# A hybrid attention and Fourier encoder on one core: banks of the reciprocal norms, request of x for the squares, place of a norm's product

## The chip, the core and the metric

The kernel runs on one core of a Trainium2 chip, as one program in one launch. TensorE (PE, with its weight loads on a row of their own, PEld), VectorE (DVE), ScalarE (ACT), GpSimd (POOL) and SyncE (SP) each work through their own list of instructions and wait for one another through semaphores. SP, POOL and ACT also issue the transfers between memory and the core; those wait in their issuer's list like any other instruction. The metric is the device time of one execution in microseconds, the median of several runs.

## What is computed

Two inputs of 1024 channels, one of 2048 tokens and one of 512, go through two layers and a final norm:

```python
def attention_layer(x, g, w_in, w_out, sink, rel_bias):
    h = rmsnorm(x, g)
    z = h @ w_in                       # q, k, v and gate in one projection
    ...
    o = banded_gqa_with_sink(q, k, v, rel_bias, sink)   # |i-j| <= 128, 16 heads, 4 kv heads
    return x + (o * jax.nn.silu(gate)) @ w_out

def fourier_layer(x, g, w_gate, w_out):
    h = rmsnorm(x, g)
    hg = h.astype(jnp.float32).reshape(b, s, N_FGROUPS, FGROUP_CH)
    f = jnp.fft.fftn(hg, axes=(1, 3), norm="ortho").real
    gate = h @ w_gate
    return x + (f.reshape(b, s, d) * jax.nn.silu(gate)) @ w_out
```

where `rmsnorm(x, g)` is `x * rsqrt(mean(x*x) + 1e-6) * g`. The sum of squares needs x with tokens on the partitions; the first projection needs x with channels there.

## The kernel before

**Products.** Operands are split into a high and a low part, and `matmul3` (line 92) multiplies high by high, high by low and low by high into one bank of accumulators (PSUM). All its matmuls show as line 95, whatever they compute; the tile names tell them apart: qp and gp (query and gate projections), op (output projection of attention), W, Z and X (gate products of the Fourier layer), z (transform over channels).

**Banks.** There are eight banks of 128x512 floats. In the attention phase four of them, `spt[0]` to `spt[3]`, are fixed and hold the scores; the other four rotate under the tag "bank" and are handed out by `bank(name)` (line 77) to qp, gp, pt, av, ib and op in turn. A tile that asks for a bank gets one of the four, and its first write waits until the previous holder has been read for the last time.

**Attention phase.** The tokens are worked through in five chunks of 512 (`CHUNKS`, line 35: first the sample's, then four of the prompt). For each chunk a loop over n = 0 to 16 (line 843) runs a pipeline over eight head pairs with two pairs of 128-query blocks each: scores of step n into `spt[:2]`, then into `spt[2:]` (line 468); DVE adds the bias and takes the minimum (`biased`, L487); ACT takes exponentials (L495); the weights are transposed (L527), copied out by ACT and DVE in two parts (`parts`, L535 and L536), and multiplied with the values in the next step (`av`, L553), whose result ACT and DVE take out (`out_evac`, L562 and L571). Pieces of the next projections are laid between as filler for TensorE. The order of PE, ACT and DVE in this loop is written out by `seq` and `pe`, which chain instructions; what isn't chained is placed by the planner that lays out the program, which takes instructions in the order in which they are written as far as its own estimate of the times has them ready.

The next chunk's reciprocal norms are made inside the same loop by `extra(i)` with i from 4n to 4n+3 (line 827):

- `stats(c)` (line 158) gives a list of steps that are taken at i = 38, 40, ... (from the second chunk on). Step `one(i)` squares the tile of x that step i-1 requested, on ACT with a running sum (L169), and requests tile i (L177). There are five tiles of 128 tokens for a chunk with a halo of 128 tokens, four for the last chunk. For chunks after the second (`c > 1`) the square is chained into ACT's order. The tiles have the tag "x", four buffers, shared with the weight sums that `EXTRA` makes up to i = 37 (w32e, e) and with the transposed x of the next chunk (xk, L212).
- `inv_rms` (line 86) makes the reciprocal roots with DVE and POOL.
- `spread(c, inv)` at i = 56, so in step n = 14, turns the column of 128 reciprocal norms of each tile into a row that is the same on all partitions: a PE transpose of the broadcast column per tile (L196) into a bank called ib, four tiles to a bank, and an ACT copy to `invb` per bank (L197). For the sample's chunk it uses `spt[0]` instead (`place`).

After the last gate projection of a chunk (`evac_g`, line 410: ACT tanh L413, DVE product L415, which is the last reader of gp's bank), step n = 14 holds av, then the spread, then the first four steps of `out_proj` (line 587), whose accumulator op takes a bank.

**Fourier phase.** The tokens are in twenty tiles, two to a `Pair`. The loop at line 1263 runs `gates(pr, hooks)` for one pair and, through the hooks, the transposes and transform of the next. For the pair after that one, x is loaded (L987), squared (L967), rooted (L88, L89) and multiplied in place by its reciprocal norm and by g (`norms`, line 989, the product at L992) at the head of each turn; the transposes L1000 read that product in the next turn. `z_odd_even` (line 1054) transforms the second tile of a pair: four banks, each read by an ACT copy (L1071) and by a DVE multiply-add (L1072). `z` (line 1035) then transforms the first tile into two further banks of the same pool of five. After every second pair, `combine` adds and subtracts four transforms on DVE (L1167).

Of the kernel before, what the change touches and what calls it, by code (L numbers as in the profile page):

```python
# [9 lines left out]
F32 = mybir.dt.float32  # L10
# [4 lines left out]
ALU = mybir.AluOpType  # L15
# [4 lines left out]
P = 128  # L20
D = 1024
# [21 lines left out]
def encoder(  # L43
# [3 lines left out]
    PE, ACT, DVE, POOL, SP = nc.tensor, nc.scalar, nc.vector, nc.gpsimd, nc.sync  # L47
# [29 lines left out]
    def bank(name):  # L77
        return banks[-1].tile([P, 512], F32, tag="bank", name=name)

    def xtile(shape, dtype, name):  # L80
        return xp.tile(shape, dtype, align_bytes=LINE, tag="x", bufs=4, name=name)
# [4 lines left out]
    def inv_rms(ss, n, name, place=lambda ins: None):  # L86
        inv = main.tile([P, 8], F32, tag="inv", bufs=2, name=name)
        place(DVE.tensor_scalar(inv[:, :n], ss[:, :n], 1.0 / D, EPS, ALU.mult, ALU.add))  # L88
        POOL.tensor_tensor(inv[:, :n], inv[:, :n], mhalf[:, :n], ALU.pow)  # L89
        return inv  # L90
# [44 lines left out]
    def after(ins, anchor):  # L135

        if anchor is not None:
            tc.add_manual_dep(ins.ins, anchor.ins.name, ISSUE, reason="issue order")

    def seq(engine, ins):  # L140

        after(ins, chain.get(engine))
        chain[engine] = ins
        return ins
# [4 lines left out]
    def attention_phase():  # L149

        with ExitStack() as es:
# [6 lines left out]
            def stats(c):  # L158

                tok, lo_t, hi_t = CHUNKS[c]  # L160
                nt = min(640, hi_t - tok) // P
                ss = main.tile([P, 8], F32, tag="ss", bufs=2, name=f"ss{c}")

                xs = []

                def one(i):

                    if i:
                        sq = ACT.activation(xs[i - 1], xs[i - 1], AF.Square, accum_out=ss[:, i - 1 : i])  # L169

                        if c > 1:
                            seq(ACT, sq)
                        else:
                            after(sq, last_exp[0])
                    if i < nt:
                        xs.append(xtile([P, D], F32, f"xs{c}_{i}"))
                        after(SP.dma_start(xs[i], x[tok + i * P : tok + (i + 1) * P, :]), last_exp[0])  # L177

                return [lambda i=i: one(i) for i in range(nt + 1)] + [
                    lambda: inv_rms(ss, nt, f"inv{c}", lambda ins: seq(DVE, ins) if c > 1 else None)  # L180
                ]

            def spread(c, inv, place=None):

                tok, lo_t, hi_t = CHUNKS[c]
                nt = min(640, hi_t - tok) // P
                if c:
                    invb = ap.tile([P, 640], F32, tag="invb", name=f"invb{c}")
                else:

                    invb = main.tile([P, 512], F32, tag="xr", bufs=3, name=f"invb{c}")
                for i0 in range(0, nt, 4):
                    m = min(4, nt - i0)
                    ps = bank(f"ib{c}_{i0}") if place is None else place
                    for i in range(m):
                        PE.transpose(ps[:, i * P : (i + 1) * P], inv[:, i0 + i : i0 + i + 1].to_broadcast([P, P]), ident)  # L196
                    ACT.copy(invb[:, i0 * P : (i0 + m) * P], ps[:, : m * P])  # L197
                return invb
# [39 lines left out]
            ps = bank("idle")  # L238
# [40 lines left out]
            spt = []  # L279
# [12 lines left out]
            last_exp, last_evac, last_mul, last_lo = [None], [None], [None], [None]  # L292
# [7 lines left out]
            def kv_proj(c, hs, halo, norms=None, early=None):  # L300
# [50 lines left out]
                for i0 in range(0, len(blocks), 4):  # L351
                    group = blocks[i0 : i0 + 4]
                    ps = [bank(f"vp{c}_{i0}_{i}")[:, :256] for i in range(len(group))]
                    for k in range(KD):
                        for i, (src, c0, b) in enumerate(group):
                            matmul3(ps[i], cols(src[k], c0, P), wslice(wv, k, 0, 256), k == 0, k == KD - 1)
                        if norms is not None and k == 4:

                            invb = spread(c, inv, spt[0])
                    for i, (src, c0, b) in enumerate(group):  # L360
                        v = ap.tile([P, 4, 2, HD], F32R, align_bytes=LINE, tag="v", bufs=6, name=f"v{c}_{b}")
                        vp = ps[i].rearrange("p (g d) -> p g d", g=4)
                        sc = 0.5
                        if inv is not None:
                            sc = ap.tile([P, 1], F32, tag="vsc", bufs=2, name=f"vsc{c}_{b}")
                            DVE.tensor_scalar(sc, inv[:, i : i + 1], 0.5, None, ALU.mult)
                        ACT.activation(v[:, :, 0, :], vp, AF.Copy, scale=sc)
                        DVE.scalar_tensor_tensor(v[:, :, 1, :], vp, sc, f32(v[:, :, 0, :]), ALU.mult, ALU.subtract)  # L368
                        vblk[b] = v
# [416 lines left out]
            for c in range(len(CHUNKS)):  # L786
# [33 lines left out]
                m = 15 * KD - ahead_n  # L820
# [6 lines left out]
                def extra(i):  # L827
                    nonlocal norm_steps, invb, inv
                    if c + 1 < len(CHUNKS):
                        if i == 24:  # L830
                            norm_steps = stats(c + 1)
                        if i >= (38 if c else 24) and i % (2 if c else 4) == 0 and norm_steps:
                            inv = norm_steps.pop(0)()
                        elif i == 56:
                            invb = spread(c + 1, inv)
                    if c in EXTRA and i in EXTRA[c]:
                        EXTRA[c][i]()
                    if c == len(CHUNKS) - 1 and i in AHEAD:
                        AHEAD[i]()
                    if c == 0 and i % 8 == 3 and 1 <= i // 8 < 3:  # L840
                        load_w(0, LATE[i // 8 - 1], f"late{i // 8}", late=last_exp[0])
# [76 lines left out]
    def fourier_phase(tail):  # L918
        with ExitStack() as es:
# [3 lines left out]
            gb = fp.tile([P, D], F32, tag="gb", bufs=1, name="g1b")  # L923
# [11 lines left out]
            def zt(name):  # L935
                return right([P, D], F32, name)
# [27 lines left out]
            def sumsq(src, name):  # L964
                ss = main.tile([P, 8], F32, tag="ss", bufs=2, name=f"ss{name}")
                junk = fp.tile([P, 512], F32, tag="c12", bufs=1, name=f"jk{name}").bitcast(BF16)
                ACT.activation(junk, src, AF.Square, accum_out=ss[:, 0:1])  # L967
                return inv_rms(ss, 1, f"inv{name}")
# [10 lines left out]
            class Pair:  # L979
# [9 lines left out]
                def norms(self, i):  # L989
                    xt = self.x[i]  # L990
                    inv = sumsq(xt, f"b{self.ts[i]}")
                    DVE.scalar_tensor_tensor(xt, xt, inv[:, 0:1], gb, ALU.mult, ALU.mult)  # L992

                def turn(self, i, hf):

# [58 lines left out]
                def z_odd_even(self):  # L1054

                    t = self.ts[1]
                    self.zs[1] = zt(f"z{t}")
                    for g in range(4):
                        ps = bank(f"z{t}_{g}")
                        for odd, m in enumerate((self.S[1], self.diff)):  # L1060

                            to = ps[:, odd * 256 : odd * 256 + 256].rearrange("p (a n) -> p a n", a=2)
                            for part in range(2):
                                PE.matmul(
                                    to, m[part][:, g * P : (g + 1) * P], ch[:, 0, :, odd * P : (odd + 1) * P],
                                    start=part == 0, stop=part == 1,
                                )
                        v = ps.rearrange("p (o a n) -> p a o n", o=2, a=2)
                        out = self.zs[1][:, g * 256 : g * 256 + 256].rearrange("p (n o) -> p o n", o=2)
                        scale = 1.0 if t >= SEQ // P else 0.5  # L1070
                        ACT.activation(out, v[:, 1], AF.Copy, scale=scale)  # L1071
                        DVE.scalar_tensor_tensor(out, v[:, 0], scale, out, ALU.mult, ALU.add)  # L1072

            def prod(out, a, b, ks, first):

# [492 lines left out]
            for i, l in enumerate((w0, w2)):  # L1568
                for a in range(3):
                    t = zt(f"ev{a}_{i}")  # L1570
# [5 lines left out]
            def pm(a, b, name):  # L1576

                n = zt(name)
                tt(n, a, b, A)
                tt(a, a, b, S)  # L1580
                return n, a
# [5 lines left out]
            f, g4s = pm(w0[1], w0[3], "f0")  # L1587
# [14 lines left out]
            for a in range(4):  # L1602
                for i, l in enumerate((pc, qs)):
# [3 lines left out]
                    t = zt(f"od{a}_{i}")  # L1607
# [170 lines left out]
```

## Time and profile before

| | |
|---|---|
| median of 3 runs | 1596.12 us (1593.97 to 1597.15) |
| the profiled execution | 1597.6 us, its span 1595.8 us |
| granted TensorE clock | 0.999 |
| attention phase, about | the first 1075 us of the span |
| Fourier phase, about | the rest |
| x requested for squares (L177) | 23 transfers of 512 KB, median 6.2 us from issue to landing |

The profile is one execution. PE is busy when a matmul is in the array; matmuls overlap, so the mean duration of one is longer than the distance from one to the next. In the timeline each row gives the start, the time over which a merged group ran, engine, line, operation, output and inputs with shapes, a count, and in brackets how long the engine had been idle before it and what ended that. "PE op L95 <- DVE s L415" in the view of waits is read as: TensorE, about to do line 95 into tile op, waited for DVE's line 415 on tile s.

### The profile page before, as it was taken

What the parts mean: (1) busy time and instruction counts of PE and PEld (TensorE: products, weight loads), DVE (VectorE), ACT (ScalarE), POOL (GpSimd) and SP (SyncE); (2) the same over time, 40 slices, a digit from 0 to 9 for tenths busy, and PEclk for the clock granted to TensorE, in tenths of its full rate; (3) what the DMA queues carried; (4) which work ended last, traced back from release to release, by engine and by line L of the source; (5) the groups of instructions that cost most, each with busy time, mean ns of one, the idle gap of its engine ahead of it and who ended that gap; (6) DMA issues with size and microseconds to landing.
All of it is one profiled execution on the core that took longest, in us unless ns stands there. A gap on an engine that the chain in (4) does not pass through costs nothing. (4 is left out here: it accounts for less than half of the span.)

```text
span 1595.8 us, 27413 instructions
## 1 busy us (share of the span) xinstructions
PE 1576.0 (99%) x9743; PEld 1320.9 (83%) x9743; DVE 1152.2 (72%) x2785; ACT 875.0 (55%) x2088; POOL 446.9 (28%) x613
## 2 busy tenths in 40 slices
PE   9999999999999999999999999999999999999998
PEld 7878788888888878988888888888888888888886
DVE  6788665887548775377764587769778878889796
ACT  6688534676237774257752476646555554243242
POOL 2466652421404314024223242123112111110110
PEclk9999999999999999999999999999999999999999
DMA  7598695565856566756659655675557469558762
GB/s 295 191 325 286 222 352 212 216 229 207 299 213 216 209 233 236 245 191 239 234 166 328 229 205 216 247 252 200 205 204 256 171 220 404 184 178 308 264 206 79
DMA packets 100579, 373.88 MB, mean 234 GB/s; under 512 B 12139, under 2 KB 22379, under 8 KB 83036
## 3 DMA queue, kind: packets, MB, share of 16 engines
q1 hardware_dynamic: 81708, 297.91, 53.0%
q0 software_dynamic: 16400, 70.04, 11.4%
q10 hardware_dynamic: 2336, 4.20, 0.7%
q8 instruction: 77, 1.26, 0.3%
q14 instruction: 58, 0.48, 0.1%
HBM read 280.84 MB, written 91.26 MB: 233 GB/s over the span
## 5 line engine op out<-in xcount | busy, mean ns | idle before, releaser
L487 DVE CUSTOM_DVE_ANT_0 S<-spt,b 128x385 f32<-128x385 f32 (+1 forms) x320 | 156.0, 527 | 113.7 <-PE spt L468 72.8
L95 PE MATMUL qp<-h,wq 128*128 128x512 f32 x960 | 237.4, 396 | 0.3 <-DVE v L368 0.2
L95 PE MATMUL gp<-h,wg 128*128 128x512 f32 x960 | 237.5, 395 | 0.0
L95 PEld LDWEIGHTS qp<-h,wq 128*128 128x128 f32 x960 | 174.9, 188 | 37.6 <-DVE v L368 0.8
L95 PEld LDWEIGHTS gp<-h,wg 128*128 128x128 f32 x960 | 174.9, 188 | 37.1 <-issue 1.0
L495 ACT ACTIVATE S<-S 128x385 f32<-128x385 f32 (+1 forms) x320 | 188.8, 597 | 19.1 <-DVE S L487 18.6
L535 ACT CAST pts<-pt 128x384 fp32r<-128x384 f32 (+1 forms) x240 | 100.4, 462 | 171.5 <-PE pt L527 163.9
L536 DVE TENSOR_TENSOR pts<-pt,pts 128x384 fp32r<-128x384 f32 (+1 forms) x240 | 114.6, 523 | 27.7 <-ACT pts L535 27.6
L577 POOL TENSOR_TENSOR uT<-o,uT 128x256 fp32r<-128x256 f32 x75 | 55.6, 741 | 245.2 <-ACT uT L576 245.2
L95 PE MATMUL op<-wo,uT 128*128 128x512 f32 x480 | 119.0, 392 | 3.0 <-DVE s L415 3.0
L95 PE MATMUL spt<-wo,uT 128*128 128x512 f32 x480 | 120.4, 391 | 0.0
L553 PEld LDWEIGHTS av<-pts,v 128*128 128x128 f32 x576 | 100.9, 188 | 23.2 <-DVE pts L536 2.9
L553 PE MATMUL av<-pts,v 128*128 128x512 f32 (+1 forms) x576 | 117.5, 343 | 1.7 <-DVE pts L536 1.0
L468 PE MATMUL spt<-kwin,qab 64*128 64x384 f32 (+1 forms) x960 | 118.5, 352 | 0.0
L95 PE MATMUL fo<-wo,tTu 128*128 128x512 f32 x480 | 115.3, 392 | 0.0
L95 PEld LDWEIGHTS op<-wo,uT 128*128 128x128 f32 x480 | 89.3, 188 | 22.3 <-DVE s L415 3.8
L95 PEld LDWEIGHTS spt<-wo,uT 128*128 128x128 f32 x480 | 89.1, 188 | 18.4
L507 DVE TENSOR_SCALAR S<-S 128x384 f32<-128x384 f32 (+1 forms) x192 | 97.8, 510 | 6.8
L95 PEld LDWEIGHTS fo<-wo,tTu 128*128 128x128 f32 x480 | 88.3, 188 | 17.2 <-ACT wo L1534 0.3
L468 PEld LDWEIGHTS spt<-kwin,qab 64*128 64x128 f32 x960 | 74.6, 186 | 28.4 <-issue 27.5
L573 POOL TENSOR_TENSOR o<-o,s 128x256 f32<-128x256 f32 x75 | 55.3, 738 | 132.3 <-DVE o L571 132.0
L527 PE MATMUL pt<-ident,S 64*128 64x64 f32 x1344 | 82.6, 222 | 0.0
(322 smaller groups left out, 3182.1 us busy)
## 6 DMA issues: line engine op xcount, KB each, us to landing
wo<-wsd SPq DMA_DIRECT2D x32, 1024.0 KB, 5.1
wq<-wsd SPq DMA_DIRECT2D x31, 1024.0 KB, 7.3
wg<-wsd SPq DMA_DIRECT2D x31, 1024.0 KB, 4.9
x<-x1d SPq DMA_DIRECT2D x40, 512.0 KB, 3.9
b<-b21d SPq DMA_DIRECT2D x40, 512.0 KB, 6.5
b<-rowd SPq DMA_DIRECT2D x40, 384.0 KB, 4.1
xs<-in_x_dram SPq DMA_DIRECT2D x23, 512.0 KB, 6.2
s2d<-gt POOLq DMA_DIRECT2D x40, 256.0 KB, 5.2
```

The lines of the kernel that those rows point to most:

```text
L95: pe(PE.matmul(out, a[i], b[j], start=start and i + j == 0, stop=stop and i == 1, skip_group_check=more))
L468: pe(PE.matmul(banks[j][:, 2 + k0 * P : 2 + k1 * P], res["q"][rows, qp, b * P : (b + 1) * P], kwin[g][rows, kp, b * P + k0 * P : b * P + k ...
L487: seq(DVE, DVE.tensor_tensor_reduce(out=s[:, e0:e1], in0=ps[:, 1 + e0 : 1 + e1], in1=st["bias"][:, j, 386 - e1 : 386 - e0][:, ::-1], scale ...
L495: last_exp[0] = seq(ACT, ACT.activation(s[:, e0:e1], s[:, e0:e1], AF.Exp, bias=s[:, 386:387], scale=-1.0, accum_out=s[:, 387:388]))
L507: seq(DVE, DVE.tensor_scalar(s[:, ks], s[:, ks], den, None, ALU.mult))
L527: pe(PE.transpose(ps[h][:, kb, j, :], ss[j][rows, 1 + kb * P : 1 + (kb + 1) * P], ident[rows, rows]))
L535: seq(ACT, ACT.copy(hi, ps[:, k0:k1]))
L536: seq(DVE, DVE.tensor_tensor(lo, ps[:, k0:k1], f32(hi), ALU.subtract))
L553: pe(PE.matmul(to, v, pt, start=n == part == 0, stop=part == 1 and n in (1, len(todo) - 1), skip_group_check=n > 1,))
L573: eng.tensor_tensor(o, o, s, ALU.mult)
L577: low = eng.tensor_tensor(lo, o, f32(hi), ALU.subtract)
```

## The change

Three edits.

1. `spread` no longer takes rotating banks. It cuts the tiles three and two (or three and one in the last chunk) instead of four and one, and writes them into columns 2 to 385 of `spt[3]` and `spt[2]`. The sample's chunk goes on as before.
2. In `stats`, for chunks after the second, the first step requests two tiles of x, and each later step requests the tile after the next, until all are requested.
3. In the Fourier phase the product L992 is placed on DVE behind the last L1072 that was written before it: an edge that orders two instructions of one engine and adds no semaphore.

```diff
-                    if i < nt:
-                        xs.append(xtile([P, D], F32, f"xs{c}_{i}"))
-                        after(SP.dma_start(xs[i], x[tok + i * P : tok + (i + 1) * P, :]), last_exp[0])
+                    while len(xs) < min(nt, i + (2 if c > 1 else 1)):
+                        t = len(xs)
+                        xs.append(xtile([P, D], F32, f"xs{c}_{t}"))
+                        after(SP.dma_start(xs[t], x[tok + t * P : tok + (t + 1) * P, :]), last_exp[0])
...
-                for i0 in range(0, nt, 4):
-                    m = min(4, nt - i0)
-                    ps = bank(f"ib{c}_{i0}") if place is None else place
+                step = 3 if place is None else 4
+                for i0 in range(0, nt, step):
+                    m = min(step, nt - i0)
+                    ps = spt[3 - i0 // 3][:, 2:386] if place is None else place
...
-                    DVE.scalar_tensor_tensor(xt, xt, inv[:, 0:1], gb, ALU.mult, ALU.mult)
+                    after(DVE.scalar_tensor_tensor(xt, xt, inv[:, 0:1], gb, ALU.mult, ALU.mult), last_z[0])
...
-                        DVE.scalar_tensor_tensor(out, v[:, 0], scale, out, ALU.mult, ALU.add)
+                        last_z[0] = DVE.scalar_tensor_tensor(out, v[:, 0], scale, out, ALU.mult, ALU.add)
+
+            last_z = [None]
```

## The prediction

> **What bounds the kernel now.** I read the page first: the engines, the granted clock in forty slices, and the projections' row of the costliest groups.
>
> ```profile
> span 1595.8 us, 27413 instructions
> PE 1576.0 (99%) x9743; PEld 1320.9 (83%) x9743; DVE 1152.2 (72%) x2785; ACT 875.0 (55%) x2088; POOL 446.9 (28%) x613
> PEclk9999999999999999999999999999999999999999
> L95 PE MATMUL qp<-h,wq 128*128 128x512 f32 x960 | 237.4, 396 | 0.3 <-DVE v L368 0.2
> ```
>
> TensorE is busy for 99% of the span at full clock in every slice, so the change, which takes no matmul away, can only give back time in which TensorE stood still: 1595.8 - 1576.0 = 19.8 us in all, its start and tail included. The last row gives the pace: 237.4 / 960 = 0.247 us from one 128x512 matmul to the next, though one lasts 0.396; a matmul that is held up therefore loses about 0.15 us more than the idle time shown. Next I read who TensorE, and then its weight loads, waited for, longest first.
>
> ```profile
> PE op L95 <- DVE s L415: 3.0, 3, 1.5
> PE z L95 <- DVE z L1072: 1.6, 2, 1.3
> PE av L553 <- DVE pts L536: 1.0, 3, 0.3
> PE W L95 <- DVE c L1138: 1.0, 1, 1.0
> PE av L553 <- ACT pts L535: 0.6, 3, 0.2
> ...
> PEld op L95 <- DVE s L415: 3.8, 3, 1.8
> PEld av L553 <- DVE pts L536: 2.9, 6, 0.7
> PEld av L553 <- ACT pts L535: 2.1, 4, 0.7
> PEld z L95 <- DVE z L1072: 2.0, 2, 1.5
> ```
>
> Three of these causes are touched: op behind s, av behind pts, z behind z. Together they are 3.0 + 1.6 + 1.0 + 0.6 = 6.2 us of PE's idle time, or 3.8 + 2.9 + 2.1 + 2.0 = 10.8 us of the weight loads'. The Trainium skill (Perfetto Trace Analysis, section Identifying the Most-Contended Engine) holds that matmul busy time misleads because matmuls are pipelined, and that the share of weight loads is to be read instead. By that rule the touched stalls are worth 10.8 us, by PE's own idle time 6.2; the sum below takes start to start, which comes out between.
>
> **Edit 1, the spread leaves the rotating banks.** The timeline of step n = 14 in three chunks, and the same place in the chunk with one ib bank:
>
> ```profile
> 169.81 2.59 PEld L95 LDWEIGHTS op<-wo,uT 128*128 128x128 f32 x12 [1.79 <-DVE s L415]
> 385.44 2.63 PEld L95 LDWEIGHTS op<-wo,uT 128*128 128x128 f32 x12 [0.87 <-DVE s L415]
> 599.13 0.55 DVE L487 CUSTOM_DVE_ANT_0 S<-spt,b 128x385 f32<-128x385 f32 x1
> 600.88 0.71 PE L196 MATMUL ib<-ident,inv 128*128 128x128 f32 x5
> 602.23 0.76 ACT L197 COPY invb<-ib 128x512 f32<-128x512 f32 x2
> 602.45 2.59 PEld L95 LDWEIGHTS op<-wo,uT 128*128 128x128 f32 x12 [1.10 <-DVE s L415]
> 606.35 0.78 PE L468 MATMUL spt<-kwin,qab 64*128 64x384 f32 x6
> 816.53 0.60 PE L196 MATMUL ib<-ident,inv 128*128 128x128 f32 x4
> 816.89 3.02 PE L95 MATMUL op<-wo,uT 128*128 128x512 f32 x12
> ```
>
> With gp, av and two ib tiles alive all four rotating banks are taken, and op waits until L415 has read gp's. With only one ib bank, at 816.89, op starts 0.36 us after the transposes began; at 602.45 it starts 602.45 - 600.88 = 1.57 after, for one transpose more, so about 1.1 is lost, which is the weight loads' idle time. I take that for the three places: 1.79, 0.87 and 1.10, 3.76 us. With the score banks a rotating bank is free, and op follows the transposes.
>
> What stands next behind the stall differs in the first chunk only, where the low part of the weight is still being made:
>
> ```profile
> 168.56 2.81 POOL L126 TENSOR_TENSOR wo<-w32o,wo 128x256 fp32r<-128x256 f32 x4 [4.01 <-ACT wo L121]
> ```
>
> Four quarters of 0.70 us end at 169.26, 169.97, 170.67 and 171.37. op would start at 169.81 - 1.79 = 168.02; its eighth matmul, the first with this weight's low half, is due 7 x 0.247 later at 169.75 and waits 0.22 for the second quarter; the eleventh, due at 170.71, waits 0.66 for the fourth. That gives 0.88 back and leaves 0.91. If the low part is awaited as a whole, the eighth waits until 171.37 and nearly all is given back (0.17 left); if POOL's work comes sooner, all 1.79 stay. I take 0.91, since the work is cut into quarters. Edit 1: 0.91 + 0.87 + 1.10 = 2.9 us, bounds 2.1 and 3.8.
>
> Its new waits are covered. The transposes wait for L487's last read of `spt[3]`, which ended at 599.68, 1.2 us ahead of them. The scores of step n = 15 into `spt[2:]` must wait for the copies: these end at 602.99, and the scores come at 606.35, or 605.25 with 1.10 gained, so 2.2 us remain; were they late, the scores and all of PE behind them would be late by as much. The copies are still two (384 and 256 columns for 512 and 128); the last chunk has one more, which is shorter than the 0.76 us of these two and lies in the same 2.2 us.
>
> **Edit 2, x a step sooner.** The third prompt chunk's statistics, with SP's issues, ACT's square and the matmuls that follow:
>
> ```profile
> 548.20 0.73 POOL L656 TENSOR_TENSOR e<-w32e,e 128x256 fp32r<-128x256 f32 x1
> 552.76 1.11 SPq L177 DMA_DIRECT2D xs<-in_x_dram  x1
> 561.51 0.81 SPq L177 DMA_DIRECT2D xs<-in_x_dram  x2
> 567.33 1.06 ACT L169 ACTIVATE xs<-xs 128x1024 f32<-128x1024 f32 x1 [2.92 <-DMA xs<-in_x_dram]
> 570.18 0.50 PE L553 MATMUL av<-pts,v 128*128 128x512 f32 x1 [0.23 <-ACT pts L535]
> 571.02 1.42 PE L553 MATMUL av<-pts,v 128*128 128x512 f32 x7 [0.33 <-DVE pts L536]
> ...
> 580.37 0.51 PE L553 MATMUL av<-pts,v 128*128 128x512 f32 x1 [0.20 <-ACT pts L535]
> 581.21 1.43 PE L553 MATMUL av<-pts,v 128*128 128x512 f32 x7 [0.33 <-DVE pts L536]
> 787.78 1.43 PE L553 MATMUL av<-pts,v 128*128 128x512 f32 x7 [0.34 <-DVE pts L536]
> ```
>
> Two requests go out in one step, and the second square, chained into ACT, is due before its tile has landed. ACT waits 2.92 us, the copies of pts behind it are late, DVE's part behind those, and av holds up TensorE twice, once for each half. Start to start that is 0.23 + 0.33 + 2 x 0.15 = 0.86 here, 0.20 + 0.33 + 0.30 = 0.83 at 580, and 0.34 + 0.15 = 0.49 at 787. Sum 2.2 us. PE's idle time alone makes 0.23 + 0.33 + 0.20 + 0.33 + 0.34 = 1.4, the lower bound; the weight loads' waits for pts in the second view are 2.9 + 2.1 = 5.0 in the whole kernel, of which not all follow a square, and I put the upper bound at 4.0. Requested at 552.76 with the first, the second tile has over 14 us until 567.33, and every later one a step of some nine; the waits should be gone.
>
> The moved issues go past others on SP: one transfer more at 552.76, the same two at 561.51, one fewer after, so a weight load behind the first is 0.4 us later, while it is needed steps later. A blocked issue would hold up all of SP; but the second buffer is free: POOL's last read of the weight rows ended at 548.93. If it were not, the load of wq behind it would wait too.
>
> **Edit 3, the product behind the copies.** Around the fifth pair's transform:
>
> ```profile
> 1177.97 1.28 DVE L992 SCALAR_TENSOR_TENSOR x<-x,invb,g1b 128x1024 f32<-128x1024 f32 x1 [0.74 <-POOL invb L89]
> 1180.37 1.42 DVE L1072 SCALAR_TENSOR_TENSOR z<-z,z 128x256 f32<-128x256 f32 x4
> 1180.85 1.70 PE L95 MATMUL z<-chan_sb,tTb 128*128 128x256 f32 x12 [1.33 <-DVE z L1072]
> 1188.54 1.03 PE L1000 MATMUL trb<-ident,x 128*128 128x128 f32 x8
> ...
> 1232.68 1.70 PE L95 MATMUL z<-chan_sb,tTb 128*128 128x256 f32 x12 [0.24 <-DVE z L1072]
> ```
>
> L992 runs 1.28 us ahead of the copies that free the banks; z's second half waits 1.33 us for the first of them. Without it the gate product between them and then L1072 come 1.28 sooner, and z follows. Gain 1.33 + 0.24 plus some 0.1 each, 1.75 us (1.6 to 2.0). The product then runs from about 1180.5 (1180.37 + 1.42 - 1.28) to 1181.8, and its reader L1000 stands at 1188.54, or 1187.1 with z's wait gone: 5.3 us of cover. Behind it on DVE are the second norm and the gates' last product, no later than now, for the order alone changes.
>
> **Sum.** 2.9 + 2.2 + 1.75 = 6.9 us; bounds 2.1 + 1.4 + 1.6 = 5.1 and 3.8 + 4.0 + 2.0 = 9.8. The profiled execution took 1597.6 (1.8 outside its span), which gives 1590.7; the median, 1.5 lower, gives 1589.2. I forecast 1590.0, between them.
>
> **Rivals.** (a) Half is given back: a planner lays out the unchained Fourier phase by its own times and, with the inputs moved, orders DVE otherwise; waits such as W's 1.0 above grow, or new ones of that size come. Three would leave 3.9 us of the sum: 1593. For it: W's is of that kind. Against: the attention loop is chained by hand. (b) The change doesn't do what it says: op still gets gp's bank, and the second square still waits, so only edit 3 is left: about 1595. Against it is 816.89, where one bank less sufficed. (c) Slower: the product L992 falls behind `combine`.
>
> ```profile
> 1157.72 1.22 DVE L1167 TENSOR_TENSOR er<-z,z 128x1024 f32<-128x1024 f32 x1
> 1161.29 1.03 PE L1000 MATMUL trb<-ident,x 128*128 128x128 f32 x8
> ```
>
> `combine` is six instructions of 1.22, written ahead of the norms. If the bound product drops behind them, it ends at 1157.72 + 7.3 + 1.28 = 1166.3, 5.0 us after its transposes are due, in four of the nine turns: 20 us lost, 1597.6 - 6.9 + 20 = 1611. It decides once the product starts after 1160.0. Against it: L1072 ends some 4 us before L1167 can begin, as that needs z. The Trainium skill (TensorE: Matmul & The Clock Gate, section Architectural detail) states that VectorE keeps strictly to its order; by that nothing would pass a product so placed. No row here tests it.
>
> **How the numbers follow.** Forecast 0.60, (a) 0.22, (b) 0.08, (c) 0.05, and 0.05 for other orders that cost a few us. The forecast's own range is 1596.1 - 9.8 = 1586.3 to 1597.6 - 5.1 = 1592.5; to hold 8 in 10 it goes up through (a) and (b) to 1595.5, and down to 1585.5. A difference under 0.2%, 3.2 us, can't be told from none; faster means below 1592.9: nearly all of the forecast and half of (a), 0.69. Same: the rest of (a), (b) and a little of the forecast, 0.20; slower 0.11, from (c), the other orders and the scatter of single runs.
>
> **What would show it.** In the new profile the wait of op for s and that of z for L1072 are gone, ACT's wait for xs (L169) has no entry after the second chunk, av's waits around 570, 580 and 787 are gone, and PE's busy time is unchanged while the span is shorter. A wait of op for POOL's L126 in the first chunk is the 0.88. The forecast is wrong if new waits of TensorE in the Fourier phase exceed 3 us, or if L1000 waits for L992.

## The result and the profile after

The changed kernel takes 1589.08 us, the median of 7 runs (1587.93 to 1590.71), beside 1595.74 (1593.49 to 1597.15) for 7 runs of the kernel before on the same chip: 6.66 us less, a ratio of 0.996 with an interval from 0.9948 to 0.9972. The forecast was 1590.0 and a gain of 6.9. The profiled execution took 1588.22 us, so the two profiled executions lie 9.4 us apart, more than the medians: before's was 1.9 above its median, and after's 0.9 under.

The page of the kernel after, its span and engines, and then the whole of its view of what PE waited for (total, times, longest; entries from 0.2 us on):

```profile
span 1586.5 us, 27419 instructions
PE 1573.1 (99%) x9743; PEld 1321.4 (83%) x9743; DVE 1153.0 (73%) x2785; ACT 874.6 (55%) x2089; POOL 445.6 (28%) x613
PE Ap L95 <- ACT gp L1310: 1.5, 1, 1.5
PE idle L242 <- DVE idle L239: 1.2, 1, 1.2
PE W L95 <- DVE c L1142: 1.0, 1, 1.0
PE spt L95 <- ACT h L220: 0.6, 1, 0.6
PE trb L1002 <- DVE xrl L637: 0.3, 1, 0.3
PE Bp L95 <- DVE up L1346: 0.3, 1, 0.3
PE Ap L95 <- DVE gp L1311: 0.3, 1, 0.3
PE Wo L95 <- DVE x L1439: 0.2, 1, 0.2
```

Line numbers are up to four higher than before (L1072 is L1074, L992 is L994, L196 is L198). The three touched causes, op behind s, av behind pts and z behind z, have no row left; the number of matmuls is the same. PE's busy time is 2.9 us less (1576.0 before) and its idle time 6.4 less (19.8 before, 1586.5 - 1573.1 = 13.4 now); the two make up the 9.3 us by which the spans differ. W's 1.0 is as it was; the only row that is new is trb's of 0.3, and the row of spt, which the change doesn't touch, went from 1.0 to 0.6.

The timeline of step n = 14 in the first of the three chunks, to be held against op's row of 169.81 with its wait of 1.79:

```profile
166.81 0.71 PE L198 MATMUL spt<-ident,inv 128*128 128x128 f32 x5
167.28 3.02 PE L95 MATMUL op<-wo,uT 128*128 128x512 f32 x12
167.89 2.83 POOL L126 TENSOR_TENSOR wo<-w32o,wo 128x256 fp32r<-128x256 f32 x4 [4.04 <-ACT wo L121]
169.23 0.76 ACT L199 COPY invb<-spt 128x384 f32<-128x384 f32 x2
171.07 0.61 PE L470 MATMUL spt<-kwin,qab 64*128 64x256 f32 x6
172.19 1.65 PE L95 MATMUL op<-wo,uT 128*128 128x512 f32 x6
```

op follows 0.47 us after the transposes began, and its twelve matmuls run through in 3.02 us, 0.25 each, while POOL is still at its four quarters until 170.72. The row of 171.07 is the scores into `spt[2:]`, that of 172.19 op's fifth and sixth steps, three matmuls each.

For the statistics, the answer on ACT's line 169 says what ACT waited for; the first row is of the kernel before, over the whole program:

```profile
  DMA xs<-in_x_dram: 10.2, 6
```

```profile
  DMA xs<-in_x_dram: 0.3, 1
```

The remaining 0.3 is the program's very first square, at 15.25 us, in the sample's chunk. Around the third prompt chunk the timeline of the kernel after shows both requests issued together and both squares back to back:

```profile
549.64 2.21 SPq L178 DMA_DIRECT2D xs<-in_x_dram  x2
...
559.61 1.06 ACT L169 ACTIVATE xs<-xs 128x1024 f32<-128x1024 f32 x1
560.57 0.19 ACT L169 ACTIVATION_READ_ACCUMULATOR xs<-xs 128x1 f32 x1
560.66 1.05 ACT L169 ACTIVATE xs<-xs 128x1024 f32<-128x1024 f32 x1
```

Around the fifth pair's transform, the order on DVE is turned, and z's 24 matmuls run as one group without a wait:

```profile
1168.74 1.41 DVE L1074 SCALAR_TENSOR_TENSOR z<-z,z 128x256 f32<-128x256 f32 x4
1170.06 1.27 DVE L994 SCALAR_TENSOR_TENSOR x<-x,invb,g1b 128x1024 f32<-128x1024 f32 x1
1170.32 3.04 PE L95 MATMUL z<-chan_sb,tTb 128*128 128x256 f32 x24
```

Starts of the same matmul in the two traces say where the time came from: the lead of the kernel after grows by 1.9 us at the first spread, 0.9 at the second and 1.2 at the third (4.0 in all), by 0.2, 1.1, 1.1 and 0.6 behind the squares (3.0), and by 1.5 and 0.5 at the two transforms of the Fourier phase (2.0). That is 9.0; another 0.6 stands already at 104 us, ahead of everything the change touches. Two traces alone cannot say how much of this would come again; the runs of the single edits can.

### The profile page after: what moved, and what is told of

Read it like the earlier page. It is cut to its first block, busy times and chain, and to the rows that moved or that the text cites. A ratio compares the mean times of both kernels' runs of the same rounds, so it can differ in the third digit from the quotient of the medians.

```text
span 1586.5 us, 27419 instructions
## 1 busy us (share of the span) xinstructions
PE 1573.1 (99%) x9743; PEld 1321.4 (83%) x9743; DVE 1153.0 (73%) x2785; ACT 874.6 (55%) x2089; POOL 445.6 (28%) x613
## 5 line engine op out<-in xcount | busy, mean ns | idle before, releaser
L529 PEld LDWEIGHTS pt<-ident,S 64*128 64x128 f32 x1344 | 79.0, 138 | 4.2 <-issue 1.9
```

The lines of the kernel that those rows point to most:

```text
L529: pe(PE.transpose(ps[h][:, kb, j, :], ss[j][rows, 1 + kb * P : 1 + (kb + 1) * P], ident[rows, rows]))
```

## The experiments

Each kernel was run beside the kernel before on the same chip; a ratio is to that kernel, with its 95% interval. An interval here is some 2 us to either side, so the waits in the trace carry the verdict where medians are close.

**The kernel before, once more.** No edit; it shows what comes again from one execution to the next.

> The kernel before once more, for a second profile. Theory: its stalls are set by the order of the instructions, so the three waits (op behind s 3.0 us, av behind pts 1.6, z behind z 1.6 of TensorE's idle time) are there again within a few tenths, and the time is 1595.7. Rival: a part of them comes from how fast a transfer landed in that one execution; then av's waits, which hang on a landing, differ by 1 us or more between the two profiles, while op's and z's stay.

Measured: 1596.22 us, ratio 1.0003 (0.9994 to 1.0012). Its view of PE's waits has these rows:

```profile
PE op L95 <- DVE s L415: 3.2, 3, 1.7
PE z L95 <- DVE z L1072: 0.9, 2, 0.6
```

The three waits of op come again (3.0 in the first profile, 3.2 here). So do av's, which follow a landing (1.0 + 0.6 there, 1.0 + 0.4 here; ACT's wait for xs 10.2 and 10.4). z's wait does not keep its size: 1.6 there, 0.9 here, in the same program. The expectation's rival had these two the other way round.

**Edit 1 alone**, the spread in the score banks:

```diff
-                for i0 in range(0, nt, 4):
-                    m = min(4, nt - i0)
-                    ps = bank(f"ib{c}_{i0}") if place is None else place
+                step = 3 if place is None else 4
+                for i0 in range(0, nt, step):
+                    m = min(step, nt - i0)
+                    ps = spt[3 - i0 // 3][:, 2:386] if place is None else place
```

> The spread in score banks alone. By the matmuls' starts in the two profiles this edit gave 1.9 + 0.9 + 1.2 = 4.0 us: 1591.7, with av's and z's waits as before. Rival, the sum on record: 2.9 us, 1592.8, the first chunk keeping 0.9 of 1.8. Second rival: the gain shows only together with the other edits, because the next step's matmuls wait for something else: 1595.

Measured: 1591.26 us, ratio 0.9972 (0.996 to 0.9984), 4.2 us under the 1595.47 of that chip's runs of before. op's wait has no row any more, as expected. What was not expected: z's wait has none either, though the product still stands ahead of the copies. The 4.2 us therefore hold whatever that wait was worth, beside op's.

**Edit 2 alone**, x a step sooner:

```diff
-                    if i < nt:
+                    while len(xs) < min(nt, i + (2 if c > 1 else 1)):
```

> The request of x a step sooner alone. By the starts this edit gave 0.2 + 1.1 + 1.1 + 0.6 = 3.0 us: 1592.7, no wait of ACT for xs after the second chunk, op's and z's waits as before. Rival, the sum on record: 2.2 us, 1593.5. Second rival: the landing was quick in other executions anyway, and the median moves by under 1 us.

Measured: 1592.8 us, ratio 0.9984 (0.9975 to 0.9993), 2.7 us under; op's wait stays at 2.8, av's waits for pts are gone; z's is 0.3.

**Edit 3 alone**, the product behind the copies:

```diff
-                    DVE.scalar_tensor_tensor(xt, xt, inv[:, 0:1], gb, ALU.mult, ALU.mult)
+                    after(DVE.scalar_tensor_tensor(xt, xt, inv[:, 0:1], gb, ALU.mult, ALU.mult), last_z[0])
```

> The order of the norm's product alone. By the starts this edit gave 1.5 + 0.5 = 2.0 us: 1593.7, z's wait for L1072 gone and L1000 waiting for nothing new. Rival: with the attention phase unchanged the planner orders the Fourier phase otherwise and the gain is 0 to 1 us.

Measured: 1596.19 us, ratio 1.0005 (0.9996 to 1.0014), no gain. z's wait is gone from its trace. The interval allows 0.0004 x 1595.5 = 0.6 us of gain at the most, and edits 1 and 2 alone add up to 4.2 + 2.7 = 6.9 us, all of the change's 6.66. Both profiles of the kernel before have the wait, 1.6 and 0.9 us, so up to a microsecond of it does not show; where that goes is open.

**The change without edit 3**, the same question from the other end:

```diff
-                    after(DVE.scalar_tensor_tensor(xt, xt, inv[:, 0:1], gb, ALU.mult, ALU.mult), last_z[0])
+                    DVE.scalar_tensor_tensor(xt, xt, inv[:, 0:1], gb, ALU.mult, ALU.mult)
```

> The changed kernel without its third edit: the norm's product is free again, the other two stay. Theory (the z stall hangs on when x lands and is mostly absent once the phase begins earlier): 1589 us, 0.9955 of before, z's wait for the copies 0.5 us or less. Rival (the third edit keeps the 1.75 us forecast): 1591, with z's wait 1.3 us or more.

Measured: 1589.15 us, ratio 0.9948 (0.9937 to 0.996), beside 0.996 (0.9948 to 0.9972) for the whole change. z's wait has no row. So with edits 1 and 2 in, edit 3 has no measurable worth.

**Why z's wait comes and goes: x made late on purpose.** In the timeline of the repeated kernel before, the same place as in the prediction:

```profile
1175.15 1.06 ACT L967 ACTIVATE jkb<-x 128x1024 bf16<-128x1024 f32 x1 [0.96 <-DMA x<-x1d]
...
1177.23 1.28 DVE L992 SCALAR_TENSOR_TENSOR x<-x,invb,g1b 128x1024 f32<-128x1024 f32 x1 [0.74 <-POOL invb L89]
...
1180.11 1.70 PE L95 MATMUL z<-chan_sb,tTb 128*128 128x256 f32 x12 [0.27 <-DVE z L1072]
```

and in that of edit 1 alone, whose square waited 0.24 us for x in place of 0.96:

```profile
1168.16 1.06 ACT L968 ACTIVATE jkb<-x 128x1024 bf16<-128x1024 f32 x1 [0.24 <-DMA x<-x1d]
...
1170.24 1.28 DVE L993 SCALAR_TENSOR_TENSOR x<-x,invb,g1b 128x1024 f32<-128x1024 f32 x1 [0.74 <-POOL invb L89]
...
1172.43 3.04 PE L95 MATMUL z<-chan_sb,tTb 128*128 128x256 f32 x24
```

The chain runs from x's landing through the square, the root and the product to the copies behind it. The next place where z waits shows it from the other end. In four executions with the product ahead of the copies (before, before again, edit 2, edit 1) the square stood idle for 1.39, 1.76, 1.40 and 0.98 us and z for 0.24, 0.61, 0.25 and not at all: z waits for what exceeds 1.15 us. The second and fourth ended with x's landing; for the other two the view names DVE's sum c (L1142), so x is not the only thing that holds the square. To test the chain, the kernel before got four copies of 2 MB that nobody reads, issued on POOL behind a group's last sum. The orders of DVE's product and copies stay as they were.

```diff
+    dump = [dram.tile([4 * P, D], F32, name=f"dump{t}") for t in range(16)]
...
+                    if last_c[0] and i:
+                        after(POOL.dma_start(dump[t], x1d[: 4 * P, :]), last_c[0])
+                        last_c[0] = None
                     queue.dma_start(self.x[i], x1d[t * P : (t + 1) * P, :])
...
-                tt(e, e, z[2], ALU.add)
+                last_c[0] = tt(e, e, z[2], ALU.add)
```

> The kernel before, with four further copies of 2 MB from memory to memory on POOL's queue (nobody reads them), one behind each group's last sum, so that the next pair's x lands later without any instruction of DVE or TensorE changing its order. Theory (L992 stands ahead of the copies on DVE, so z waits for x's landing): with x 1 to 3 us late z's wait for the copies grows from 0.9-1.6 to 4 us or more, at three places, and the time is 1599 to 1604. Rival (the wait has another cause): z's wait stays under 2 us, 1596 to 1597.

Measured: 1617.88 us, ratio 1.0134 (1.0119 to 1.0149), slower than either expectation had it, since x came later than meant. The timeline and PE's waits of this kernel:

```profile
1178.78 1.06 ACT L968 ACTIVATE jkb<-x 128x1024 bf16<-128x1024 f32 x1 [6.38 <-DMA x<-x1d]
1180.86 1.29 DVE L997 SCALAR_TENSOR_TENSOR x<-x,invb,g1b 128x1024 f32<-128x1024 f32 x1 [0.75 <-POOL invb L90]
1183.73 2.93 PE L96 MATMUL z<-chan_sb,tTb 128*128 128x256 f32 x12 [5.24 <-DVE z L1077]
1186.46 4.16 PE L96 MATMUL W<-wB,tTb 128*128 128x512 f32 x12
```

```profile
PE z L96 <- DVE z L1077: 15.9, 3, 5.8
```

x is waited for 6.38 - 0.96 = 5.4 us longer than in the run of before, and z 5.24 - 0.27 = 5.0 longer. At the other two places the square waits 6.93 and 6.03 us and z 5.78 and 4.88, the same 1.15 less. The wait comes from the landing; the rival falls.

The rest of the 21.4 us, beyond the 15.0 that z's wait grew by, is for the most part a slower clock behind the stalls. A stretch behind the first of them (its length, PE's busy time, the granted clock, DMA share, GB/s):

```profile
1184.00:1186.00 2.00, 2.00 (x10) 0.50 0.70 268
```

It was 0.50 up to 1188. In the repeated kernel before it was 1.00 from 1180 to 1184, and the W group that takes 4.16 us here took 2.91. The clock fell behind the other two stalls as well (0.50 from 1243 to 1246, 0.63 from 1301 to 1304). PE's busy time is 1580.8 us beside 1575.8, 5.0 more with the same matmuls; 15.0 + 5.0 makes 20.0 of the 20.3 by which the two spans differ (1615.0 and 1594.7).

**The same late x with edit 3:**

> The same four copies with the third edit alone. Theory: the product stands behind the copies, so a late x no longer reaches z; z's wait is 0.3 us or less, and the time lies at least 3 us under that of the late x without the edit, at 1596 to 1598. Rival: the two agree within 1 us.

Measured: 1615.47 us, ratio 1.0107 (1.0093 to 1.0121), 2.4 us under the one without the edit. The edit does help when x is late, but z waits on:

```profile
1185.43 1.06 ACT L968 ACTIVATE jkb<-x 128x1024 bf16<-128x1024 f32 x1 [6.52 <-DMA x<-x1d]
1186.48 1.13 ACT L1110 ACTIVATE gt<-c 128x512 f32<-128x512 f32 x2
1186.61 0.15 DVE L89 TENSOR_SCALAR invb<-ssb 128x1 f32<-128x1 f32 x1 [6.38 <-ACT jkb L968]
1187.13 1.29 DVE L1111 SCALAR_TENSOR_TENSOR gt<-gt,c 128x512 f32<-128x512 f32 x2 [0.36 <-ACT gt L1110]
1187.53 1.20 ACT L1076 ACTIVATE z<-z 128x256 f32<-128x256 f32 x4
1188.34 1.41 DVE L1077 SCALAR_TENSOR_TENSOR z<-z,z 128x256 f32<-128x256 f32 x4
1188.82 2.93 PE L96 MATMUL z<-chan_sb,tTb 128*128 128x256 f32 x12 [3.79 <-DVE z L1077]
```

```profile
PE z L96 <- DVE z L1077: 9.9, 3, 3.8
```

There are further ways from the landing to z that I had not seen. ACT's square of x (L968) heads ACT's list, and the gates (L1110) and ACT's own copies of z (L1076) stand behind it. On DVE the first step of the root (L89) waits for the square, 6.38 us, and the gates' products (L1111) and the copies (L1077) stand behind that; the copies also add to what ACT's copies wrote. Edit 3 moves only the product out of the way. From the start of the square to z it is 1183.73 - 1178.78 = 4.95 us without the edit and 1188.82 - 1185.43 = 3.39 with it, and 4.96 and 3.39 at the other two places: 1.57 us a place, 4.7 of the 6.0 us by which z's wait fell; the remaining 1.2 is x, which was a little less late in this execution (18.1 us of waiting squares beside 19.3). My expectation of 0.3 us was wrong in that.

Of the 6.0 us that z no longer waits, 2.4 reach the median. In the trace PE's idle time is 2.9 less (31.3 beside 34.2), since other waits grew, PE's Z for DVE (invb, L89) by 2.0 us the most, and its busy time is 1.5 more: behind the first stall, 3.79 us, the clock stood at 0.50 from 1188 to 1194. Behind the third, 2.77 us, it stayed at 1.00.

**One bank fewer** is enough for op. On the kernel before, only the fifth tile's transpose leaves the rotating banks.

```diff
-                    ps = bank(f"ib{c}_{i0}") if place is None else place
+                    ps = place if place is not None else spt[3][:, 2:130] if i0 else bank(f"ib{c}_{i0}")
```

> Only the fifth tile of the spread goes to a score bank (its columns 2 to 129 of spt 3); the first four stay in one rotating bank. Theory, the number of rotating banks held decides: op finds a free bank as in the last chunk, its wait for s is gone and about 4 us are gained: 1591.7. Rival, one ib bank is still one too many in the chunks with a halo: the wait stays and the time is 1595.7.

Measured: 1591.7 us, ratio 0.9973 (0.996 to 0.9987), as edit 1 alone; op's wait has no row. Its timeline at the first spread:

```profile
166.93 0.60 PE L196 MATMUL ib<-ident,inv 128*128 128x128 f32 x4
167.36 0.27 PE L196 MATMUL spt<-ident,inv 128*128 128x128 f32 x1
167.39 3.02 PE L95 MATMUL op<-wo,uT 128*128 128x512 f32 x12
```

The stall is the fifth holder of four banks and nothing else; where the transposes go is of no matter as long as op finds a bank free.

**The product behind `combine`**, the case of the slower rival, made by hand on the changed kernel:

```diff
             def tt(out, a, b, op):
-                DVE.tensor_tensor(out, a, b, op)
+                return DVE.tensor_tensor(out, a, b, op)
...
-                tt(e, e, z[2], ALU.add)
+                last_z[0] = tt(e, e, z[2], ALU.add)
```

> The changed kernel with the norm's product bound behind the last of combine's six sums in the turns that have them. Theory, the price named in the prediction: the product ends about 5 us after its transposes are due, in four turns, TensorE waits for L994 and 20 us are lost: 1609. Rival: TensorE has other matmuls that the planner puts ahead of the transposes, or the sums come early enough, and less than 5 us are lost: under 1594.

Measured: 1590.94 us, ratio 0.997 (0.9959 to 0.998), 1.9 us above the change and not 20; the intervals overlap, so that even the 1.9 are not shown. The timeline of this kernel, PE and DVE:

```profile
1155.24 2.88 PE L95 MATMUL W<-wT,S 128*128 128x512 f32 x12
1157.39 2.48 DVE L994 SCALAR_TENSOR_TENSOR x<-x,invb,g1b 128x1024 f32<-128x1024 f32 x2
1157.96 0.84 PE L95 MATMUL X<-b,tTb 128*128 128x512 f32 x3
1158.81 1.06 PE L1002 MATMUL trb<-ident,x 128*128 128x128 f32 x8
```

Both products run behind the last sum, and the first ends at 1158.67, where the same transposes began at 1153.68 in the kernel after: 5 us late, as priced. But in the kernel after, at 1154.47, W's twelve matmuls come behind the first eight transposes; here the planner, which lays the program out with this edge in it, has put them and X's three ahead. PE's wait for the product (trb behind x, L994) is 1.0 us in the whole program.

**Two steps sooner**, to see whether a step is enough for edit 2:

```diff
-                    while len(xs) < min(nt, i + (2 if c > 1 else 1)):
+                    while len(xs) < min(nt, i + (3 if c > 1 else 1)):
```

> The changed kernel with x requested two steps sooner: three tiles in the first step. Theory: no wait for x is left to remove, and the third tile's buffer is one whose store is still under way, so SP is blocked for some 5 us at that place in each of three chunks; what stands behind it, a projection's weights, is needed steps later, and the time stays at 1589. Rival: the weights behind the blocked request come late and TensorE waits for wq, 1 us or more in each chunk: over 1592.

Measured: 1589.07 us, ratio 0.9954 (0.994 to 0.9968): no different from the change. SP was held up as expected, 5.4 us at the longest, though by ACT's square of an earlier tile and not by a store; it cost TensorE nothing that shows.

**What is left**, on the changed kernel: first the rows of an earlier product requested on POOL's queue and not on SP's, which is Ap's wait of 1.5; then, with that, W's wait of 1.0, by moving one step of the first tile's position work.

```diff
-                    SP.dma_start(g, src)
+                    POOL.dma_start(g, src)
```

> The changed kernel with the reads of go (the spilled groups of the last positions) issued by POOL instead of SP. In both profiles Ap waits 1.4 to 1.5 us for gp, whose read stands on SP behind the store of an output. Theory: on POOL's queue the read goes out sooner and that wait goes, 1.5 us: 1587.6. Rival: POOL's own work or its slower issue takes the gain back: 1589 or more.

```diff
-                3: [lambda: first.extend(position(*one)), lambda: f_load(3)],
-                4: [lambda: f_load(4)],
+                3: [lambda: f_load(3)],
+                4: [lambda: first.extend(position(*one)), lambda: f_load(4)],
```

> The changed kernel with the product rows requested on POOL's queue, and the first tile's position work taken from the fourth to the third hook of the last pair's gates. Theory (the place where c is read decides W's wait of 1.0): that wait goes, 1586.7 us, about 1.0 under the 1587.8 of the POOL request alone. Rival (another instruction of DVE only takes its place): 1588 or more.

The diff shows the move's direction: the kernel after has the step in hook 3, this one in hook 4; the expectation's words have it the wrong way round. Measured: 1587.76 us, ratio 0.9945 (0.9928 to 0.9962) for the POOL request, and 1591.84, ratio 0.9968 (0.9956 to 0.998), with the move. In the first, Ap's wait for ACT has no row; but with SP's request it was anywhere from 0.2 (edit 3 alone) to 1.8 us (edit 1 alone), so one trace does not show that the queue took it away. Its median is the lowest of all, 1.3 us under the change, but the intervals overlap, so that it is faster is not shown either. The second takes W's wait away and brings a longer one, which cost more than it saved:

```profile
PE tru L954 <- DVE us L1348: 3.5, 1, 3.5
```

Behind that wait, too, the granted clock was 0.50, from 1327 to 1329 us (1.00 there without the move), and the sixteen transposes took 3.35 us, where two groups of eight took 1.04 each without the move. The wait grew by 3.5 - 1.0 = 2.5 and the transposes by 1.3, together 3.8 of the 4.1 us between the two medians.

## Why the prediction was right

**The bound.** The rows that name op, av and z were the right ones to sum: they went, and nothing else above 0.2 us did. That PE's busy time would stay unchanged was wrong by the 2.9 us, nearly a third of the difference of the spans. By my estimate from the projections' row (0.396 - 0.247 = 0.15 us lost by a held-up matmul beside its idle time) the eleven waits in the rows quoted make 0.15 x 11 = 1.7 of it; the rest is open.

**Edit 1, 2.9 us predicted; 4.0 in the traces, 4.2 in the medians.** The mechanism held, including that one bank less suffices. The step that failed in size is the 0.88 us given back to POOL's low part in the first chunk. I had put POOL's four quarters from 168.56 on the weight that op's first twelve matmuls read. In the changed kernel those ran without a break from 167.28, while POOL's same row ends at 170.72. In the program's order they read the weights wo 0 and 2; POOL is making wo 4, which op reads from 172.19 on, so 1.5 us are to spare. The stall was 1.79 and the lead grew by 1.9. Both measured figures lie a little above the upper bound, 3.8; the interval of the median, 2.6 to 6.4 us, is too wide to hold that against it.

**The new waits of edit 1** were covered as said, with less to spare in the first chunk than in the third, from which the 2.2 us came: in the first the copies end at 169.23 + 0.76 = 169.99 and the scores that must wait for them begin at 171.07, 1.1 us later.

**Edit 2, 2.2 us predicted; 3.0 in the traces, 2.7 in the medians.** The three places that I priced gave 2.8 (1.1, 1.1 and 0.6). A milder place near 366 us, which I left out, gave 0.2. Requesting a step sooner removed the waits, and a second step added nothing.

**Edit 3, 1.75 us predicted; 2.0 in the two traces, nothing in the medians.** The reading of the row was right: the product stands ahead of the copies, and turning them took the wait away. The step that failed is taking 1.33 + 0.24 from one execution as what the kernel loses. The wait hangs on when the square of x can start, which x's landing sets for the most part: with the product in front it was 1.6 and 0.9 in two executions of the kernel before, 0.3 with edit 2 alone, and absent with edit 1 alone and with both, one execution each. In the trace of edit 3 alone the square at the second place waited 0.97 us, under the 1.15 beyond which z would wait, so there the edit had nothing to gain in that execution. Edits 1 and 2 gave more than predicted (1.3 and 0.5 us by the medians) and edit 3 less (1.75), and these all but cancel: that the sum of 6.9 comes so near is luck, and its terms were not that good.

**The base.** From the profiled execution I had 1590.7, from the median 1589.2, and took 1590.0. The median was the right base: 1595.74 - 6.66 = 1589.08.

**The rivals.** (a) No wait of 1 us grew in the Fourier phase of the changed kernel; W's stayed 1.0. (b) op got its bank and the squares their rows; falls. (c) The order it feared did not come, and made by hand it cost 1.9 us at the most likely, a tenth of its price: four late turns were counted as if PE had nothing else to do, but the planner filled them with other matmuls. By the Trainium skill (TensorE: Matmul & The Clock Gate, section Architectural detail), VectorE keeps strictly to its order; in the run with a late x the product (1180.86) and the copies (1183.26) kept the order written, and z waited 5.24 us, which agrees.

**Idle time or weight loads.** The Trainium skill (Perfetto Trace Analysis, section Identifying the Most-Contended Engine) speaks of shares for judging headroom, not of the price of a stall; carrying it over to stalls was my step, and it led to 10.8 us from the weight loads' waits, where PE's own idle time gave 6.2. PE's idle time shrank by 6.4, and the medians say 6.66; the two traces, 9.0, lie between. By the median, PE's idle time is the nearer measure here, since z's row, 1.6 of it, does not come again whole while the pace lost beside each wait adds to it.

## What to carry to other kernels

Before a wait is priced from one profile, follow it back. One that ends in the kernel's own order (a bank that is not free) came again here (3.0 and 3.2 us); one that ends in a transfer's landing may (av's, 1.6 and 1.4) or may not (z's, 1.6 and 0.9), and only several executions give its mean. When an operand of a moved instruction comes late, look at everything that waits for it: moving one instruction leaves the ways over the others on its own engine and on the next. Price a late instruction only after asking what the planner can put in its place.

## What was not expected of the hardware

Four copies of 2 MB on another engine's queue delayed 512 KB reads where they met them: at the three places where z waits, x took 9.6, 9.8 and 9.2 us from issue to landing, 3.3, 4.4 and 3.1 in the repeated kernel before. The page of the profile counts the packets of all queues on the same 16 engines, so that they met there is likely, but it was not separated from the memory itself. And the landing varies unprovoked: ACT's wait for x ahead of the fifth pair's square was 1.61 us in the first profile of the kernel before and 0.96 in the second.

A long stall of TensorE cost more than its length. Behind the six longest waits in these traces, 3.37 to 5.78 us, the granted clock fell to between 0.50 and 0.63 for some 3 to 6 us; behind one of 2.77 it did not. Behind the longest stall that this change removes, op's of 1.55 us, it stayed at 1.00.
